# Two stores of a linear-attention kernel, each cut into three transfers of unequal height

## The chip, the core and the metric

The kernel runs on one core of one Trainium2 chip. The metric is the device time of one launch in microseconds (us). Before the change it is 127.17 us, the median of 3 runs (127.02 to 127.25).

## What is computed

Linear attention with a ReLU feature map, without softmax, in float32 at the interface: 8 x 12 = 96 heads, 512 positions, 64 features.

```python
Q_feat = np.maximum(0, Q); K_feat = np.maximum(0, K)          # (8, 12, 512, 64)
KV = np.einsum('bhkd,bhkv->bhdv', K_feat, V)                   # 64 x 64 for each head
K_sum = np.sum(K_feat, axis=2)
numerator = np.einsum('bhqd,bhdv->bhqv', Q_feat, KV)
denominator = np.einsum('bhqd,bhd->bhq', Q_feat, K_sum)
return numerator / (denominator[:, :, :, None] + 1e-10)
```

Each of Q, K, V and the output is 12.58 MB, so 37.75 MB are read and 12.58 MB written.

## The kernel before

The 96 heads are worked through in 12 "octets" of 8 heads (`NO = 12`). For an octet, Q is one tile of 128 partitions, 2048 float32 in a partition in memory; K and V are two groups of four heads each, 128 partitions x 1024. The result of an octet is the tile `o_sb`, 128 partitions x 2048 float32: a row of 8 KB per partition, 1 MB in all, which is contiguous in memory.

Loads. The first octet's K and V come as float32 through the queues of SP and ACT (`k_first`, `v_first`, lines 109 and 110). All other loads are issued by GpSimd (lines 94 and 106) and cast to bf16 on the way; they are written out in one list at the top (K, V, Q of octet 1, of octet 2, and so on) and run as far ahead as their buffers allow (6 octets of K and of V, 7 of Q) and as far as eight completion semaphores, taken in turn, let them.

Compute. For each octet TensorE forms K'V and the sums of K (line 152), ScalarE and VectorE take them out of PSUM (162), Q is transposed (173) and passed through ReLU (181, 179), the numerator is formed transposed (203), copied (205) and transposed back (230), the denominator is formed beside it (212 to 224), and `norm` (236) multiplies by the reciprocal into `o_sb`. The order of the engines' instructions is written out by hand.

Stores. `store` (line 242) issues them from SP, one transfer of 128 rows for each octet (line 249), except for the last octet, whose tile goes out as two halves of its columns (line 247), each as soon as its `norm` is done. SP does nothing else after its first load. Stores are held back: the store of octet `o` is made to wait, beside its own `norm`, until the K load of octet `o + DELAY` has landed (`DELAY = 6`), so stores 0 to 5 stand behind loads 6 to 11:

```python
        st = nc.sync.dma_start(out=Ov, in_=o_sb)
        if o + DELAY < NO:
            tc.add_manual_dep(st.ins, k_load[o + DELAY].ins.name, after_load, reason="store after load")
```

SP takes its transfers' completion semaphores in turn from eight; a transfer waits until the last user of its semaphore has landed. `o_sb` comes from a pool of `DELAY + 2 = 8` buffers, of which `k_first` and `v_first` take two at the start, so the tile of octet 8 is written only after store 0 has landed, that of octet 9 after store 1.

Of the kernel before, what the change touches and what calls it, by code (L numbers as in the profile page):

```python
# [10 lines left out]
def kernel(  # L11
# [7 lines left out]
    nc = tc.nc  # L19
    B, H, S, D = Q.shape  # L20
    assert D == 64
    P = 128
# [9 lines left out]
    NO = NG // 2  # L32
    assert NO * 8 == NH and R == 16 and RQ == 32
    DELAY = 6

    fp32 = mybir.dt.float32
    bf16 = mybir.dt.bfloat16
# [3 lines left out]
    def pool(name, bufs, **kw):  # L41
        return ctx.enter_context(tc.tile_pool(name=name, bufs=bufs, **kw))
# [6 lines left out]
    rcp = pool("rcp", 2)  # L49
    outp = pool("outp", DELAY + 2)  # L50
    otp = pool("otp", 2)
# [37 lines left out]
    k_load = {}  # L89
    after_load = mybir.DependencyInfo(mybir.DependencyClass.Sync, mybir.DependencyReason.DATA)  # L90
# [151 lines left out]
    def store(o, o_sb):  # L242
        Ov = Or[o].rearrange("p (r d) -> p r d", d=D)
        if o == NO - 1:
            for j in range(2):
                rs = slice(RQ // 2 * j, RQ // 2 * (j + 1))
                nc.sync.dma_start(out=Ov[:, rs], in_=o_sb[:, rs])
            return
        st = nc.sync.dma_start(out=Ov, in_=o_sb)
        if o + DELAY < NO:  # L250
            tc.add_manual_dep(st.ins, k_load[o + DELAY].ins.name, after_load, reason="store after load")

    def out_tile():
        return outp.tile([P, RQ, D], fp32, name="o_sb", tag="o_sb")
# [19 lines left out]
    def backs(o):  # L274
        o_sb = out_tile()
        for j in range(2):
            norm(o, j, back(o, j), o_sb)
        store(o, o_sb)
# [26 lines left out]
    o = NO - 2  # L305
# [10 lines left out]
    o_sb = out_tile()  # L316
# [4 lines left out]
    for i in range(2):  # L321
        relu_q(o + 1, i, transp(o + 1, i), nc.vector if i == 1 else None)
    norm(o, 1, ps, o_sb)
    store(o, o_sb)
    idle(5, o + 1)
    out_t(o + 1, (0,))
# [32 lines left out]
```

## Time and profile before

| | us |
|---|---|
| median of 3 runs | 127.17 (127.02 to 127.25) |
| profiled execution, device time | 127.0 |
| its span, first to last instruction | 125.2 |
| outside the span | 1.8 |
| store 0 issued on SP | 51.74 |
| store 1 issued on SP | 61.67 |
| last two stores issued on SP | 118.23 and 119.36 |

| engine | busy us | share of the span |
|---|---|---|
| TensorE matmuls | 85.0 | 68% |
| VectorE | 81.0 | 65% |
| ScalarE | 79.0 | 63% |
| GpSimd | 23.7 | 19% |
| the 16 DMA engines, mean, in 38 of 40 slices | | 90% or more |

The page cuts the span into 40 equal slices of 3.1 us. The row "DMA" gives the mean busy share of the core's 16 DMA engines in tenths (9 stands for 90% or more), the row below it what they moved. A queue's line gives its packets, megabytes, and the time that its packets took as a share of 16 engines' span: 0.4% is 0.004 x 16 x 125.2 = 8 us of one engine's time.

The trace also holds a record for each DMA packet (start, duration, size, queue, but not which engine carried it) and for each landing of a transfer: 49 transfers have 784 landing records, 16 each.

### The profile page before, as it was taken

Reading aid. Unit: us, or ns where it says so; the run is one execution under the profiler, and the core shown is the slowest. Engines: PE = TensorE matmul, PEld = TensorE weight load, DVE = VectorE, ACT = ScalarE, POOL = GpSimd, SP = SyncE. Lnnn points to the kernel's source line nnn. Section 1 sums busy time; section 2 is a strip of 40 time slices with the busy share of each in tenths; the row PEclk is TensorE's granted clock in tenths of the full one; section 3 lists DMA queues with packets and bytes.
Section 4 is the critical chain, followed back from the end, with each engine's and each line's share of the span. In section 5 each row is a group of like instructions: output and inputs, shape, how many; then the busy total and the mean of one; then the engine's idle time right before and its main releaser. Section 6 shows DMA issues by size and latency. Waiting matters only on the chain.

```text
span 125.2 us, 2614 instructions
## 1 busy us (share of the span) xinstructions
PE 85.0 (68%) x1067; PEld 76.9 (61%) x1067; DVE 81.0 (65%) x176; ACT 79.0 (63%) x114; POOL 23.7 (19%) x40
## 2 busy tenths in 40 slices
PE   0000547898989979898966985955997597797600
PEld 0000547796878879787855983943975595775500
DVE  2006963679889797979859349449549409978610
ACT  0003737999899898989877576845499095547000
POOL 6922124221242213322121130210000000000000
PEclk9999999999999999999999599996899869999996
DMA  3999999999999999999999999999999999999991
GB/s 92 365 306 229 215 209 211 213 211 217 207 217 208 211 213 211 214 273 311 214 247 341 210 222 342 234 217 325 258 215 305 279 215 307 425 419 419 432 403 73
DMA packets 10139, 32.66 MB, mean 261 GB/s; under 512 B 784, under 2 KB 784, under 8 KB 8720
## 3 DMA queue, kind: packets, MB, share of 16 engines
q0 software_dynamic: 7712, 17.83, 74.1%
q1 hardware_dynamic: 2144, 13.63, 27.1%
q10 hardware_dynamic: 272, 1.05, 2.2%
q8 instruction: 8, 0.13, 0.4%
q14 instruction: 3, 0.02, 0.0%
HBM read 37.75 MB, written 12.58 MB: 402 GB/s over the span
## 4 chain that ended last, share of the span: by engine, by line
DVE 37%; DMA 28%; PE 19%; ACT 7%; issue 3%; DVEq 1%; ACTq 0%
DMA v_sb<-in_V_dram 20%; DVE o_sb L236 15%; PE ps_kv L152 10%; DMA k_first<-in_K_dram 7%; DVE kf L138 7%; PE ps_bk L230 7%; DVE vo L140 4%; ACT kvd L162 3%; DVE vo L147 3%; DVE den L220 2%; PE ps_qt L173 2%; DVE rec L224 2%; DVE own L215 2%; ACT qt L181 2%; ACT vo L145 1%
## 5 line engine op out<-in xcount | busy, mean ns | idle before, releaser
L152 PE MATMUL ps_kv<-vo,kf 128*128 128x132 bf16 x384 | 30.2, 240 | 19.9 <-ACT vo L145 13.8
L152 PEld LDWEIGHTS <-kf 128*128 128x128 bf16 x384 | 27.4, 107 | 21.6 <-DVE vo L140 12.9
L236 DVE TENSOR_TENSOR o_sb<-ps_bk,rec 128x1024 f32<-128x1024 f32 x24 | 28.3, 1219 | 13.6 <-PE ps_bk L230 13.6
L162 ACT CAST kvd<-ps_kv 64x260 bf16<-64x260 f32 (+1 forms) x54 | 18.6, 345 | 16.6 <-PE ps_kv L152 13.9
L205 ACT COPY ot_sb<-ps_ot 128x1024 f32<-128x1024 f32 x24 | 24.1, 1013 | 6.8 <-PE ps_ot L203 5.9
L230 PE MATMUL ps_bk<-ident,ot_sb 128*128 128x128 f32 x192 | 23.4, 276 | 0.4 <-ACT ot_sb L205 0.4
L181 ACT ACTIVATE qt<-ps_qt 128x1024 bf16<-128x1024 bf16 x23 | 22.4, 1028 | 0.2
L230 PEld LDWEIGHTS ps_bk<-ident,ot_sb 128*128 128x128 f32 x192 | 21.2, 143 | 0.7 <-ACT ot_sb L205 0.7
L203 PE MATMUL ps_ot<-qt,kvd 128*128 128x256 bf16 x96 | 14.9, 283 | 9.9 <-DVE o_sb L236 9.0
L138 DVE TENSOR_SCALAR kf<-k_sb,mask 128x1024 bf16<-128x1024 bf16 x44 | 18.4, 459 | 4.5 <-DMA k_sb<-in_K_dram 4.5
L203 PEld LDWEIGHTS <-kvd 128*128 128x128 bf16 x96 | 9.2, 100 | 13.2 <-issue 11.0
L173 PE MATMUL ps_qt<-ident,q_sb 128*128 128x128 bf16 x192 | 14.7, 237 | 0.7 <-DMA q_sb<-in_Q_dram 0.7
L173 PEld LDWEIGHTS <-q_sb 128*128 128x128 bf16 x192 | 13.3, 108 | 1.4 <-DMA q_sb<-in_Q_dram 1.3
L140 DVE TENSOR_SCALAR vo<-v_sb,mask 128x1024 bf16<-128x1024 bf16 x22 | 11.0, 501 | 4.7 <-DMA v_sb<-in_V_dram 4.7
L145 ACT ACTIVATE vo<-v_sb,mask 128x1024 bf16<-128x1024 bf16 x10 | 11.5, 1154 | 2.0 <-DMA v_sb<-in_V_dram 1.8
L94 POOL DMA_DIRECT2D v_sb<-in_V_dram x11 | 8.2, 750 | 22.2 <-DMA q_sb<-in_Q_dram 9.4
L106 POOL DMA_DIRECT2D q_sb<-in_Q_dram x12 | 7.1, 588 | 20.9 <-DMA k_sb<-in_K_dram 15.3
L94 POOL DMA_DIRECT2D k_sb<-in_K_dram x11 | 7.9, 717 | 15.4 <-DMA v_sb<-in_V_dram 9.8
L212 PEld LDWEIGHTS <-qt 128*128 128x128 bf16 x192 | 6.8, 96 | 3.6 <-ACT qt L181 2.5
L212 PE MATMUL ps_den<-kvd,qt 128*128 128x16 bf16 x192 | 7.3, 180 | 1.9 <-ACT qt L181 1.7
L145 ACT ACT_TABLE_LOAD x1 | 1.3, 1283 | 11.3 <-DMA v_first<-in_V_dram 11.3
L138 DVE TENSOR_SCALAR kf<-k_first,mask 128x1024 bf16<-128x1024 f32 x4 | 2.8, 750 | 7.7 <-DMA k_first<-in_K_dram 7.7
(24 smaller groups left out, 31.8 us busy)
## 6 DMA issues: line engine op xcount, KB each, us to landing
out_dram<-o_sb SPq DMA_DIRECT2D x11, 1024.0 KB, 8.9
q_sb<-in_Q_dram POOLq DMA_DIRECT2D x12, 512.0 KB, 20.7
k_sb<-in_K_dram POOLq DMA_DIRECT2D x11, 512.0 KB, 21.8
v_sb<-in_V_dram POOLq DMA_DIRECT2D x11, 512.0 KB, 20.5
k_first<-in_K_dram SPq DMA_DIRECT2D x1, 1024.0 KB, 9.3
v_first<-in_V_dram ACTq DMA_DIRECT2D x1, 1024.0 KB, 10.5
out_dram<-o_sb SPq DMA_DIRECT2D x2, 512.0 KB, 4.5
```

What stands on the lines that cost most here:

```text
L94: ld = eng.dma_start(out=t.rearrange("p g r d -> p g (r d)"), in_=X[2 * o:2 * o + 2].rearrange("g p f -> p g f"))
L138: nc.vector.tensor_scalar(kf[g][:, :, s, :], k_sb[g], scalar1=0.0, scalar2=mask[:, 0, s:s + 1], op0=Alu.max, op1=Alu.mult)
L140: nc.vector.tensor_scalar(vo[g % NB][:, :, 0, 2:D + 2], v_sb[g], scalar1=mask[:, 1, 0:1], scalar2=None, op0=Alu.mult)
L152: nc.tensor.matmul(ps_kv[:, g % 2, 0:2 * (D + 2)].rearrange("p (t d) -> p t d", t=2), kf[g][:, r, :, :].rearrange("p s d -> p (s d)"), vo[ ...
L162: copy(kvd[o % NK][64 * c:64 * c + 64, 4 * gs.start + s:4 * gs.stop:2, c * D1:c * D1 + D1].rearrange("p (g t) d -> p g t d", t=2), ps_kv[6 ...
L173: nc.tensor.transpose(ps[:, u, :], q_sb[o][:, i * (U // 2) + u, :], ident)
L181: nc.scalar.activation(to, ps, Act.Relu)
L203: nc.tensor.matmul(ps[:, i], kvd[o % NK][:, h, 1:2 * D + 1], q[:, :, h, :], start=True, stop=True, skip_group_check=True)
L205: nc.scalar.copy(ot[o][:, :, 4 * j:4 * j + 4], ps.rearrange("p h u c -> p u h c"))
L212: nc.tensor.matmul(ps[:, u], qt_sb[o % NZ][:, u, :], kvd[o % NK][:, :, 0:2 * D1:2 * D1 - 1], start=True, stop=True, skip_group_check=True)
L230: nc.tensor.transpose(ps[:, 2 * v:2 * v + 2].rearrange("p c d -> p (c d)"), ot[o][:, 8 * j + v].rearrange("p h c -> p (h c)"), ident32)
L236: nc.vector.tensor_tensor(o_sb[:, rs], ps, rec[o][:, rs].unsqueeze(2).to_broadcast([P, 16, D]), op=Alu.mult)
```

## The change

The stores of octets 0 and 1 are each cut along the partitions into three transfers, issued one after the other on SP: 112, 8 and 8 rows for octet 0; 112, 12 and 4 rows for octet 1. All other stores stay as they are. Each piece is given the same dependence on the K load of `o + DELAY`. The purpose that the change states is that low-numbered DMA engines carry more rows than high-numbered ones.

```diff
     DELAY = 6
+
+    SPLIT = {0: (112, 8, 8), 1: (112, 12, 4)}
...
-        st = nc.sync.dma_start(out=Ov, in_=o_sb)
-        if o + DELAY < NO:
-            tc.add_manual_dep(st.ins, k_load[o + DELAY].ins.name, after_load, reason="store after load")
+        at = 0
+        for n in SPLIT.get(o, (P,)):
+            st = nc.sync.dma_start(out=Ov[at:at + n], in_=o_sb[at:at + n])
+            at += n
+            if o + DELAY < NO:
+                tc.add_manual_dep(st.ins, k_load[o + DELAY].ins.name, after_load, reason="store after load")
+        assert at == P
```

In the built program the streams of TensorE, ScalarE and GpSimd are unchanged. SP issues 17 transfers instead of 13 after its first load; of three pieces only the first carries the wait for the K load and for `norm`, the other two follow it directly. The `norm` of octet 8 waits for three completion semaphores where it waited for one, and so does that of octet 9. As SP takes four semaphores more, some later stores wait for other transfers than before (store 4 for the first piece of store 0, store 10 for store 2); the last two wait for stores 3 and 4 as before.

## The prediction

> **What bounds the kernel now.** I read the page's rows by slice first, because a change to stores can only matter if the DMA engines matter.
>
> ```profile
> DMA  3999999999999999999999999999999999999991
> GB/s 92 365 306 229 215 209 211 213 211 217 207 217 208 211 213 211 214 273 311 214 247 341 210 222 342 234 217 325 258 215 305 279 215 307 425 419 419 432 403 73
> q8 instruction: 8, 0.13, 0.4%
> ```
>
> The 16 DMA engines are busy from the second slice to the last but one, while no compute engine passes 68% of the span. The third line is a small queue that will carry the argument: 8 packets of 16 KB, in which the chip fetches instructions. Their 0.4% of 16 engines' 125.2 us is 8 us, so about 1 us each (in the packet records 0.88 to 0.97 us). They come at 27, 37, 48, 58, 71, 83, 98 and 112 us.
>
> Next the stages, to see whether the end is compute or the draining of stores (columns: busy us and count of each engine, clock, DMA share, GB/s), and the last issues on SP.
>
> ```profile
> 100.00:107.00 7.00, 5.63 (x58) 5.12 (x57) 3.82 (x6) 5.22 (x8) 0.00 (x0) 0.82 1.08 272
> 107.00:120.00 13.00, 9.50 (x115) 8.38 (x114) 9.80 (x18) 4.87 (x10) 0.00 (x0) 1.00 1.01 423
> 120.00:122.00 2.00, 0.00 (x0) 0.00 (x0) 0.00 (x0) 0.00 (x0) 0.00 (x0) 1.00 0.98 404
> ```
>
> ```profile
> 118.23 1.46 SPq L247 DMA_DIRECT2D out_dram<-o_sb  x2
> ```
>
> From 107 us on only stores move, at 423 GB/s with all engines full; compute is over at 119.3 us and the last store is issued at 119.36. From issue to first packet an idle queue took 1.07 us (`k_first`: issued at 0.74, first packet at 1.81), and a half tile takes an engine 1.25 us (8 packets of 156 ns). An engine without backlog would thus end at 119.36 + 1.07 + 1.25 = 121.68. The actual ends are in the DMA rows from 120 to 126 us (40 slices of 0.15 us):
>
> ```profile
> DMA  9998899999998767554421000000000000000010
> GB/s 492 382 437 355 355 410 382 410 437 410 410 410 328 300 273 273 218 218 191 164 109 55 27 0 0 0 0 0 0 0 0 0 0 0 0 0 0 0 55 0
> ```
>
> The engines do not stop together: they drop out one after the other from 121.8 to 123.5 us. The last engine sets the end: its landing is recorded at 123.89, and 1.3 us later the span is over. So the kernel ends when the most loaded DMA engine has worked off its share.
>
> **Which engine is last, and why.** The records do not name a packet's engine, but an engine's packets follow each other closely: one starts 3 to 22 ns before the end of the one before it. Following the packets from the end of the run backward, with the known order of each engine's transfers (8 rows per 1 MB store and one 4-byte completion, and so on), gives 16 chains without an idle gap of more than 25 ns from 13 us to the end. All 16 carry the same data at the same pace (a 2 KB load packet takes 173 ns on nearly all of them). Their ends differ by the fetches: each of the eight hits another chain. The eight chains without one end at 121.80, 121.82, 121.86, 121.91, 122.10, 122.32, 122.53 and 122.74; the eight with one at 122.94, 122.94, 123.02, 123.09, 123.23, 123.23, 123.35 and 123.56. The landing records agree: behind each fetch one more of a load's 16 landings is about 1 us late.
>
> What moves per row: within the draining stage an 8 KB row starts 306 ns after the one before it (309 ns long, 3 ns overlap). As no engine idles, a row taken off an engine at 52 or 62 us ends that engine's work 0.31 us earlier at 123 us, and a row added ends it 0.31 us later.
>
> **The change part by part.**
> Rows. Before, each engine carries 8 rows of each store. If a transfer is spread by number from engine 0 up, one row in turn, 112 rows are 7 on each engine, 8 rows are one on engines 0 to 7, 12 one on 0 to 11, 4 one on 0 to 3. Over both stores engines 0 to 3 carry 9 + 9 = 18 rows (+2, +0.61 us), 4 to 7 carry 9 + 8 = 17 (+1, +0.31), 8 to 11 carry 7 + 8 = 15 (-1, -0.31), 12 to 15 carry 7 + 7 = 14 (-2, -0.61). The trace has no transfer of fewer than 128 rows, so this spread is an assumption. The Trainium skill ("DMA: Bandwidth & Descriptors", section on why a DMA increments its semaphore by 16) says the same for the queues of SP and ACT: the largest count up to 16 that divides the rows, on the lowest-numbered engines; no run here shows it yet.
>
> Are the eight late engines the high-numbered ones? `k_first` is issued to idle engines, and their first packets start one after the other, 1.81 to 2.04 us, some 14 ns apart. If that order is the engines' number, the last nine starters are engines 7 to 15. Followed back to there, 6 or 7 of these nine are late chains and only 1 or 2 of the first seven. Chains cross between 3 and 13 us, where some links are guesses, so I take this as evidence and not as proof: three chances in four.
>
> Then the eight late chains gain 0.31 or 0.61. The latest, 123.56, ends at 123.25 if it is one of engines 8 to 11 and at 122.95 if not. The other eight lose 0.31 or 0.61: the one at 122.74 ends at 123.05 or 123.35, the one at 122.53 at 122.84 or 123.14. The last engine thus ends between about 123.0 and 123.35 instead of 123.56: a gain of 0.2 to 0.55 us. I take 0.4, the middle.
>
> Issue. Four more transfers on SP at 0.33 us each (row of the stores, 332 ns), 1.3 us in all. They stand behind stores 0 and 1 on a queue whose next own wait, for the K load, lasts until 61.7 and 71.6 us: nothing late. SP waits 98.5 us for K loads in all, which is the cover; without it the price is 0.33 us each. Completion packets: 4 bytes, 6 to 22 ns each, two to four more on an engine, under 0.1 us. Waits: the `norm` of octets 8 and 9 waits for three landings instead of one, but store 0 landed at 60.7 and store 1 at 69.7, over 20 us before those tiles are written, and VectorE's queue behind them isn't touched. The semaphores taken in turn by stores 4 and 10 belong to transfers that landed tens of us before.
>
> A rule against the change: the same page of the skill advises (section "Rules for kernel authors") against splitting into small transfers, with a fixed cost of about 2 us each. If that occupied the engines, four transfers would cost some 8 us (an estimate from that page). The row speaks otherwise: with engines always full, a transfer's end occupies an engine for one packet of 6 to 22 ns.
>
> Slower rows. Seven partitions per engine instead of eight may make engines meet at the same partitions' path. No row shows it; the nearest are rows of 326 to 361 ns that one chain showed while draining, against 309. With 14 rows at 0.03 to 0.05 us that is 0.4 to 0.7 us at most on an engine and perhaps nothing; I take nothing and keep 0.1 to 0.2 for the range.
>
> Compute. Loads land when the slowest engine lands, so earlier late engines bring the wait for the V load that ends at 83.97 forward by up to 0.3 us. The last store may be issued that much earlier; but the end is set by backlog, 123.56 against 121.68, so this pays nothing more.
>
> **Sum.** Profiled execution: 127.0 (span 125.2, 1.8 around it), less 0.4 is 126.6. The median of the runs is 0.17 above the profiled one: 127.17 - 0.4 = 126.77, about 126.75. Less than 0.2%, 0.25 us, is about what a measurement of this kernel can't tell from no change (three runs span 0.23 us).
>
> **Rivals.**
> Wrong half (17%): the late engines are the low-numbered ones, or a mixture. For it: the chains' early links. Against: 6 or 7 of 9. The last chain gains 1 or 2 rows: 123.56 + 0.31 to 0.61, so 127.5 to 127.8, slower. It decides as soon as the chain that ends at 123.56, or one within 0.3 us of it, is among engines 0 to 7.
> Not spread (8%): the small transfers go over one engine, or slow rows down. One engine with 7 + 8 + 8 rows of store 0 carries 15 more, 4.6 us, which even on the earliest chain passes the end by 2.8 us: 130 us or more. Mild forms end near 127.2 to 127.5.
> Compute bound (within the first case): if the end hung on the last issue at 119.36, balancing would give nothing, 127.2. The drain view speaks against it: 1.9 us lie between 121.68 and 123.56.
>
> **How the numbers follow.** Planned spread with late high engines: 75%, of which 60 exceed 0.25 us (gains of 0.2 to 0.55, small costs off), 14 lie within, 1 is slower. Wrong half: 17%, of which 14 slower and 3 within. Not spread: 8% slower. Faster 0.60, same 0.17, slower 0.23. Range: 126.45 (gain of 0.55 plus 0.17 of run scatter) up to 127.55, which takes in the weaker half of the wrong-half case; what is left out is under 2 in 10. The likeliest case's own range is 126.45 to 127.05.
>
> **What would show it.** Right: the DMA rows from 120 us on stay full longer and then fall in about 1.3 us instead of 1.75, the queue of SP counts four transfers of 32 to 112 rows more, the last landing comes near 123.5, and the instruction queue still has 8 packets of about 1 us. Wrong: the fall is longer than before (wrong half), a single engine's tail after 124 (not spread), or idle DMA slices before 121 us. A fetch that falls on other engines from run to run would undo the forecast too.

## The result and the profile after

The change makes the kernel slightly slower: 127.34 us, the median of 12 runs (127.23 to 127.57), against 127.09 (12 runs of the kernel before, taken beside them). The ratio is 1.0021, its 95% interval 1.0012 to 1.0029. The forecast was 126.75, a gain of 0.4 us. The profiled execution took 127.23 us with a span of 125.44 (before: 127.0 and 125.21), so it shows the loss at its full size: 0.23 us.

From the page after, the rows by slice of the DMA engines and the queues (packets, MB, share of 16 engines' time):

```profile
DMA  3999999999999999999999999999999999999991
...
q1 hardware_dynamic: 2176, 13.63, 26.8%
...
q8 instruction: 8, 0.13, 0.4%
q14 instruction: 3, 0.02, 0.0%
```

The engines are as full as before and the eight large instruction fetches are there. The queue of SP and its kin (q1) has 32 packets more than the 2144 of before. Four transfers that reached all 16 engines would add 64 completion packets; 32 is 8 + 8 + 12 + 4, one for each row of the small pieces. The line of q14, three small instruction fetches of 8 KB, also stood on the page before, and the prediction passed over it.

The pieces in the list of DMA issues after (transfers, KB each), and then, from the landing records, how many landings each left:

```profile
out_dram<-o_sb SPq DMA_DIRECT2D x2, 896.0 KB, 8.1
...
out_dram<-o_sb SPq DMA_DIRECT2D x2, 64.0 KB
out_dram<-o_sb SPq DMA_DIRECT2D x1, 96.0 KB
out_dram<-o_sb SPq DMA_DIRECT2D x1, 32.0 KB
```

```
112 rows: 16 landings        8 rows:  8 landings and 1 record at its issue (52.74 us)
                            12 rows: 12 landings and 1 record at its issue (62.72 us)
                             4 rows:  4 landings and 1 record at its issue (63.06 us)
```

So the spread over k engines is as the prediction assumed. It is what the Trainium skill ("DMA: Bandwidth & Descriptors", section on why a DMA increments its semaphore by 16) states, with the count that the rows divide; that the k engines are the lowest-numbered is that page's word alone, since no record names an engine. Below, "engines 0 to 3" means the four that carry two rows more, and so on.

The stages after 100 us, in the same columns as before:

```profile
100.00:107.00 7.00, 5.71 (x63) 5.18 (x61) 3.75 (x6) 5.16 (x8) 0.00 (x0) 0.85 1.08 267
107.00:120.00 13.00, 9.50 (x115) 8.38 (x114) 9.87 (x18) 4.93 (x10) 0.00 (x0) 1.00 1.02 425
120.00:122.00 2.00, 0.00 (x0) 0.00 (x0) 0.00 (x0) 0.00 (x0) 0.00 (x0) 1.00 0.97 397
```

Nothing has moved in the stages (423 GB/s became 425). The draining end, DMA rows from 120 to 126 us after:

```profile
DMA  6989999999999878642221000000000000000001
GB/s 273 437 355 464 410 410 437 382 437 410 437 410 382 328 328 355 273 191 109 109 82 82 0 0 0 0 0 0 0 0 0 0 0 0 0 0 0 0 0 55
```

The engines stay full some 0.3 us longer and then fall more steeply, in about 1.3 us. That is the sign that the prediction named for "right". Yet the last landing is recorded at 123.88, where it was at 123.89. The last engine's data did end 0.10 us earlier (its last packet of a store ends at 123.46, before at 123.55), but the landing is recorded 0.43 us behind that packet, where it was 0.34 before and is 0.33 to 0.36 in the traces of the experiments. For the rest, only the middle moved together.

**Where 0.23 us were lost: behind the last landing.** What SP waits for from 100 us on, before and then after (total us, times, longest):

```profile
SPq L354 <- DMA out_dram<-o_sb: 3.8, 3, 1.4
```

```profile
SPq L360 <- DMA out_dram<-o_sb: 4.0, 3, 1.6
```

Line 354, 360 after, issues nothing: it is the end of the program, where SP waits for every DMA completion semaphore before its first `DRAIN` instruction. The single records of that line, taken from the trace (start us, semaphore waited for; each record names a second one besides, left out here):

```
before: last store -> semaphore 117, last landing 123.89
  106 119.742 | 108 119.811 | 109 119.873 | 113 119.937 | 114 119.998 | 115 121.433 | 116 122.704 | 117 123.907
  118 123.968 | drain 124.033
after:  last store -> semaphore 113, last landing 123.88
  106 119.808 | 108 121.445 | 109 122.677 | 113 123.899
  114 123.961 | 115 124.020 | 116 124.082 | 117 124.141 | 118 124.203 | drain 124.268
```

The order is fixed, and each wait takes about 0.061 us though its semaphore is long complete. Transfers take the semaphores in turn. Before, the last store's was the last but one, so one wait stood behind it; with four transfers more it takes a semaphore four places further on in the turn of eight, which is near the front of the order, and five waits stand behind it. From last landing to first drain it is 0.143 us before and 0.385 after. The difference, 0.24 us, is as large as the whole loss: the last landing has not moved, so all of the loss lies behind it. That the last landing has not moved is itself a balance of two effects, as the experiments show.

### The profile page after: what moved, and what is told of

The parts are those of the page before. It is cut to its first block, busy times and chain, and to the rows that moved or that the text cites. A ratio compares the mean times of both kernels' runs of the same rounds, so it can differ in the third digit from the quotient of the medians.

```text
span 125.4 us, 2620 instructions
## 1 busy us (share of the span) xinstructions
PE 85.0 (68%) x1067; PEld 77.4 (62%) x1067; DVE 81.2 (65%) x176; ACT 78.9 (63%) x114; POOL 23.5 (19%) x40
## 4 chain that ended last, share of the span: by engine, by line
DVE 39%; DMA 28%; PE 20%; ACT 5%; issue 2%; DVEq 1%; ACTq 0%
DMA v_sb<-in_V_dram 20%; DVE o_sb L238 17%; PE ps_kv L154 10%; DMA k_first<-in_K_dram 7%; PE ps_bk L232 7%; DVE kf L140 7%; DVE vo L142 4%; DVE vo L149 3%; DVE den L222 2%; ACT kvd L164 2%; PE ps_qt L175 2%; DVE rec L226 2%; DVE own L217 2%; ACT qt L183 2%; DVEq L360 1%
## 5 line engine op out<-in xcount | busy, mean ns | idle before, releaser
L154 PE MATMUL ps_kv<-vo,kf 128*128 128x132 bf16 x384 | 31.0, 244 | 20.8 <-ACT vo L147 13.8
L154 PEld LDWEIGHTS <-kf 128*128 128x128 bf16 x384 | 28.2, 109 | 22.3 <-DVE vo L142 12.9
L205 PE MATMUL ps_ot<-qt,kvd 128*128 128x256 bf16 x96 | 14.0, 271 | 9.2 <-DVE o_sb L238 8.5
```

Of the source, the lines that this page charges most:

```text
L154: nc.tensor.matmul(ps_kv[:, g % 2, 0:2 * (D + 2)].rearrange("p (t d) -> p t d", t=2), kf[g][:, r, :, :].rearrange("p s d -> p (s d)"), vo[ ...
L205: nc.tensor.matmul(ps[:, i], kvd[o % NK][:, h, 1:2 * D + 1], q[:, :, h, :], start=True, stop=True, skip_group_check=True)
```

## Experiments

All kernels replace the store of one transfer by a loop over pieces; each is named by its two tables (columns are in units of 64 float32, 32 to a row). Tables that are not given are empty. After the first kernel the diffs show the table alone.

```diff
-        st = nc.sync.dma_start(out=Ov, in_=o_sb)
...
+        at = 0
+        for n in ROWS.get(o, (P,)):
+            c0 = 0
+            for c in COLS.get(o, (RQ,)):
+                st = nc.sync.dma_start(out=Ov[at:at + n, c0:c0 + c], in_=o_sb[at:at + n, c0:c0 + c])
...
```

In the table, "gap" is the time from the last landing to SP's first drain, "landing" the last landing, both in the profiled execution; "behind" is the number of waits behind the last store's. The gap is also called the exit. The kernel before ran at 126.98 to 127.02 us beside these runs, but at 127.09 beside the change, so the ratios compare better than the times.

| kernel | transfers more | behind | gap us | landing us | median us | ratio (95%) |
|---|---|---|---|---|---|---|
| before | 0 | 1 | 0.143 | 123.89 | 127.0 | 1 |
| the change | 4 | 5 | 0.385 | 123.88 | 127.34 | 1.0021 (1.0012 to 1.0029) |
| one_more | 1 | 0 | 0.082 | 123.80 | 127.13 | 1.0006 (0.9996 to 1.0016) |
| two_more | 2 | 7 | 0.511 | 123.83 | 127.46 | 1.0043 (1.0030 to 1.0057) |
| cols_4more | 4 | 5 | 0.385 | 124.42 | 127.75 | 1.0073 (1.0043 to 1.0103) |
| rows_lane | 8 | 1 | 0.143 | 124.53 | 127.66 | 1.0046 (1.0034 to 1.0058) |
| rows_lane_8k | 8 | 1 | 0.143 | 123.83 | 127.00 | 1.0004 (0.9995 to 1.0012) |
| rows_balanced | 4 | 5 | 0.384 | 123.43 | 126.87 | 0.9990 (0.9981 to 0.9998) |
| one_more_8k | 1 | 0 | 0.081 | 123.56 | 126.56 | 0.9962 (0.9948 to 0.9975) |
| low4_last | 9 | 0 | 0.081 | 124.15 | 127.23 | 1.0022 (1.0013 to 1.0030) |
| rows_bal_lane | 8 | 1 | not read | not read | 126.75 | 0.9981 (0.9972 to 0.9990) |
| low4_four | 16 | 1 | not read | not read | 130.36 | 1.0267 (1.0253 to 1.0281) |
| one_later | 1 | 0 | 0.082 | 123.62 | 126.68 | 0.9968 (0.9947 to 0.9988) |
| nine_more | 9 | 0 | 0.081 | 123.58 | 126.63 | 0.9969 (0.9956 to 0.9981) |
| no_cut | 0 | 1 | 0.143 | 123.97 | 127.06 | 1.0004 (0.9994 to 1.0013) |
| one_drain | 1 | 0 | 0.081 | 124.81 | 127.59 | 1.0049 (1.0033 to 1.0065) |
| lane_half | 8 | 1 | 0.142 | 123.74 | 126.86 | 0.9988 (0.9978 to 0.9998) |
| lane_nine | 9 | 0 | 0.081 | 124.16 | 127.19 | 1.0013 (1.0005 to 1.0022) |
| one_more_8k_again | 1 | 0 | 0.081 | 123.65 | 126.50 | 0.9963 (0.9950 to 0.9977) |
| one_later_again | 1 | 0 | 0.082 | 123.74 | 126.62 | 0.9970 (0.9958 to 0.9982) |

The profiled executions of rows_bal_lane and low4_four took 428.41 and 136.12 us, far from their medians, so their traces are not read.

### Is it the place of the last store's semaphore?

**one_more** and **two_more** cut store 0 by columns, so that no engine's rows change.

```diff
+    COLS = {0: (16, 16)}
```

> Store 0 as two column halves of 128 rows: one transfer more, so the last store takes the semaphore that SP waits for last of all. Exit theory: one wait fewer behind the last landing than before, -0.06 us, about 127.03, which the rounds may not tell from no change; in the profile 0.06 us less between the last landing and SP's last drain. Row theory, and a theory that each further transfer costs something by itself: no change, or +0.02 to +0.06 us.

```diff
+    COLS = {0: (16, 8, 8)}
```

> Store 0 as three column pieces of 128 rows: two transfers more, so the last store wraps around to the first of SP's eight completion semaphores. Exit theory: six more waits of 0.061 us follow its landing than before, +0.37 us, about 127.46, more than the change lost although only two transfers were added. Theory that each further transfer costs something (0.06 us each, as +0.25 for four would give): +0.12 us. Row theory: no change.

The gaps came as the order of waits says: no wait behind gives 0.082 us, seven give 0.511, and the steps fit 0.061 us each (0.082 + 7 x 0.061 = 0.51). The waits of SP in two_more, which is stuck at one semaphore to the end and then goes through seven:

```profile
SPq L364 <- DMA out_dram<-o_sb: 5.5, 1, 5.5
```

One transfer more is free here, two cost 0.46 us, of which the exit is 0.37 (0.511 less 0.143). The gain of 0.06 that one_more should show is not seen (127.13 against 127.0): cutting by columns has a price of its own, as the next two kernels show.

**cols_4more** was to give the change's four transfers without its moved rows, **rows_lane** the change's rows with the wheel turned on by four more.

```diff
+    COLS = {0: (16, 8, 8), 1: (16, 8, 8)}
```

> Stores 0 and 1 go out as three column pieces each, all of 128 rows: four transfers more, as in the change, but every DMA engine carries the bytes that it carried before. Exit theory: at the end SP waits for the completion semaphores one by one, some 0.06 us each, in a fixed order; four transfers more move the last store to a semaphore that stands four places earlier in that order, so four more waits follow its landing. That gives +0.24 us over the kernel before (127.09 becomes about 127.33), as large as the whole loss of the change. Row theory: the loss comes from rows that were moved onto engines which end late; with rows balanced the time is that of before, within 0.05 us.

```diff
+    ROWS = {0: (112, 8, 8), 1: (112, 12, 4)}
+    COLS = {2: (8, 8, 8, 4, 4)}
```

> The change's row pieces in stores 0 and 1, and store 2 cut into five column pieces of 128 rows: eight transfers more in all, so the last store takes the same completion semaphore as before the change. Exit theory: the end sequence is as short as before, what is left is the effect of the moved rows, which the two traces put at 0 to -0.2 us: 126.9 to 127.1. Row theory: the rows are as in the change, so the loss stays: +0.25 us, about 127.34.

The gaps are those of five waits and of one, but both ended about 0.5 us too late: pieces of columns make packets of 4, 2 or 1 KB instead of 8. Counted as time, the bytes that all engines together had moved fall behind those of before by 0.1 to 0.17 us after a store in halves (one_more), by about 0.25 after each store in 16, 8 and 8 (cols_4more), and by 0.5 to 0.6 after the one in five pieces (rows_lane), and never catch up. These two runs are confounded and decide nothing more.

**rows_lane_8k** repeats rows_lane with whole rows in store 2.

```diff
+    ROWS = {0: (112, 8, 8), 1: (112, 12, 4), 2: (32, 32, 32, 16, 16)}
```

> The change's row pieces in stores 0 and 1, and store 2 in five balanced row pieces (32, 32, 32, 16, 16): eight transfers more, whole 8 KB rows, so the last store takes the same completion semaphore as before the change. Exit theory: the end sequence is as short as before and what remains is the moved rows: 0 to -0.2 us, 126.85 to 127.1. Row theory: +0.25 us, 127.34.

Its DMA rows from 120 to 126 us:

```profile
DMA  9799999999999878543200000000000000000200
```

The change's moved rows with the exit of before run at 127.00, before at 127.02, and the gap is 0.143 again. With the exit of before the loss is gone: that the change pays 0.24 us at the exit is shown. And the moved rows, together with the cuts that move them, bring nothing of the 0.4 us forecast: the fall is steep, but the last landing stays at 123.83. Rows and cuts are taken apart further below.

### Why do the moved rows bring nothing?

The change makes engines distinguishable in the trace: a chain of packets can only belong to engines 0 to 3 if it carries two rows more, and so on. With this the 16 chains of the profile after can be put into four groups, most probably so (the assignment of one fetch, at 70.5 us, is open between the last two groups):

```
engines     rows  end of the last data packet, us           instruction fetches
0 to 3      +2    122.42  122.46  122.80  123.46            the three of 8 KB, at 29, 49 and 119 us
4 to 7      +1    122.09  122.67  123.07  123.34            two of 16 KB, at 48 and 58 us
8 to 11     -1    121.76  122.69  122.81  123.35            three of 16 KB, at 71, 84 and 98 us
12 to 15    -2    121.86  122.68  122.71  122.81            three of 16 KB, at 27, 37 and 112 us
```

Six of the eight large fetches are on the upper half, two on engines 4 to 7; engines 0 to 3 have none, but they have the small ones. The small one at 119 us costs 0.31 us for itself and 0.35 for the slow row right behind it (662 ns instead of 309); behind the one at 49 us no slow packet shows. The engine that ends last, at 123.46, is the one of engines 0 to 3 with the fetch at 119 us: without its two rows it would end at 122.85 (123.46 less 0.61). The latest engine got 0.10 us earlier, a former early one took its place, and the mean of the 16 ends hardly moved (122.65 before, 122.69 after).

The table also shows an order: taken by time, the large fetches go round the engines, 48 and 58 us on engines 4 to 7, then 71, 84 and 98 on engines 8 to 11, then 112 on engines 12 to 15, where those at 27 and 37 us had been too. The traces of rows_lane_8k and lane_nine, read in the same way, show the same round with another start (on engines 4 to 7 the fetches at 27 and 37 us in the one, at 70 and 83 in the other). Each time two fall on engines 4 to 7, three on each of the upper groups and none on engines 0 to 3. Which fetch an engine gets thus differs between these traces; how many each group gets does not.

**low4_last** was to use this: rows of store 0 to engines 0 to 3 alone, which seemed free of fetches, and the last store's semaphore at the end of the order.

```diff
+    ROWS = {0: (112, 4, 4, 4, 4), 1: (32, 32, 16, 16, 16, 16)}
```

> Store 0 as 112, 4, 4, 4, 4 rows, so engines 0 to 3 carry three rows more and all others one less, and store 1 as six balanced row pieces (32, 32, 16, 16, 16, 16): nine transfers more, so the last store takes the semaphore waited for last. The trace of the change put no instruction fetch on engines 0 to 3 and all eight on 4 to 15. If so, these twelve engines end 0.31 us earlier, the first four 0.92 later (at 122.7 to 123.1): the last landing moves from 123.9 to about 123.6, and with 0.06 us less at the exit the time is -0.2 to -0.4 us, about 126.75. If the fetches fall elsewhere (on engines 0 to 3 too), the last landing moves to 124.5 or later and the time is +0.5 us.

It ran at 127.23, and this reason fell. Its DMA rows from 120 to 126 us show a single engine's tail:

```profile
DMA  9698989999989887754120000000000000000002
```

That engine is one of engines 0 to 3 with the small fetch at 110.8 us, ending at 123.81; the three others of its group end at 122.76 to 123.17. The small fetches in the table above were taken into account only after this run.

**low4_four** measures the price of a row on these engines at a large dose.

```diff
+    ROWS = {0: (112, 4, 4, 4, 4), 1: (112, 4, 4, 4, 4), 2: (112, 4, 4, 4, 4), 3: (112, 4, 4, 4, 4)}
```

> Stores 0 to 3 each as 112, 4, 4, 4 and 4 rows: engines 0 to 3 carry 11 rows of each, twelve more than before in all, and engines 4 to 15 carry 7, four fewer. Sixteen transfers more, the last store's semaphore as before (0.14 us). If a row is worth 0.306 us on its engine wherever it was moved, engines 0 to 3 end 12 x 0.306 = 3.67 us later than the 121.8 to 122.9 at which they end without moved rows: chain ends 125.5 to 126.5, last landing 125.8 to 126.9, a time of 129.0 to 130.0 us. The DMA row from 122 us on then stays near a quarter (four of 16 engines) for some 3 us. If the small transfers were spread otherwise or rows could be made up for elsewhere, the time stays below 128.5.

Twelve rows cost 3.36 us of time, 0.28 us each; if the latest of these engines would otherwise end 0.7 us before the last, as in the table of chains, it is (3.36 + 0.7) / 12 = 0.34. Against the evenly cut rows_bal_lane of the next section (126.75) the two figures are 0.30 and 0.36. The price of 0.306 lies within all this. A row added to an engine is paid in full at the end of the kernel.

### Against cuts that move no row

**rows_balanced** and **one_more_8k** cut along rows in multiples of 16, so that every engine still has 8 rows of each store.

```diff
+    ROWS = {0: (64, 32, 32), 1: (64, 32, 32)}
```

> Stores 0 and 1 as row pieces of 64, 32 and 32: four transfers more as in the change, whole 8 KB rows as in the change, but heights that sixteen divides, so every DMA engine should carry eight rows of each store as before. This is the cut of column pieces again without their smaller packets, which had cost DMA time by themselves. Exit theory: the last landing comes as before (123.9 us in the profile), four more waits of 0.061 us follow it: +0.24 us, 127.25 to 127.35. Row theory: rows are balanced, so the time is that of before.

```diff
+    ROWS = {0: (64, 64)}
```

> Store 0 as two balanced row halves of 64: one transfer more, so the last store takes the semaphore that SP waits for last. Exit theory: one wait of 0.061 us fewer behind the last landing, -0.06 us. Row theory, and a price per transfer: no change or +0.06 us.

The exits are as computed (0.384 and 0.081), but both kernels are about 0.4 us faster than the exit alone would make them: 127.02 + 0.24 is 127.26 for the first, which ran at 126.87, and 127.02 - 0.06 is 126.96 for the second, which ran at 126.56. So the baseline for the moved rows is not the uncut store but the evenly cut one. rows_balanced is the twin of the change itself: same number and place of transfers, same exit, only the rows of stores 0 and 1 even. It runs at 0.9990 of before and the change at 1.0021, so the moved rows cost some 0.4 us here. Its DMA rows from 120 to 126 us:

```profile
DMA  9889999999987556552100000000000000001000
```

Its last landing is at 123.43, that of the change at 123.88, that of before at 123.89. The last landing of the change stands still because an even cut brings it forward by 0.46 us and the unevenness takes 0.45 of that back. So the loss of 0.24 us has the exit as its place, but not as its only remedy: with the exit of before the changed rows run at 127.00, and with even rows the longer exit is more than made up, at 126.87.

Two further pairs of twins were run in the same way. rows_bal_lane is the twin of rows_lane_8k, lane_nine that of nine_more, and lane_half has one store of each.

```diff
+    ROWS = {0: (64, 32, 32), 1: (64, 32, 32), 2: (32, 32, 32, 16, 16)}
```

> Stores 0 and 1 as 64, 32 and 32 rows and store 2 as 32, 32, 32, 16 and 16 rows: eight transfers more, so that the last store has the same completion semaphore as in the kernel before and the same number of waits behind it (0.14 us from the last landing to the first drain). It is the twin of rows_lane_8k (127.00 us), with the same number and place of transfers, but every engine carries 8 rows of each store. If the unevenly moved rows cost what separates the change from the balanced cut (about 0.4 us), this runs at 126.6 us and its last landing comes near 123.4. If the moved rows neither cost nor gain, it runs at 127.0 like its twin, and the 0.4 us of the balanced cut belongs to something else.

```diff
+    ROWS = {0: (64, 32, 32), 1: (64, 32, 32), 2: (32, 32, 32, 16, 16), 3: (64, 64)}
```

> The cuts of rows_bal_lane and of one_later together: nine transfers more, every engine 8 rows of each store, the last store's semaphore last in the order of waits (0.08 us). If each balanced cut of a store brings 0.4 us by itself, this falls to 126 us or below; if one cut brings the 0.4 once, 126.55; if the cuts bring nothing, 126.95. It is the candidate for a version that beats both kernels.

```diff
+    ROWS = {0: (112, 8, 8), 1: (112, 12, 4), 2: (32, 32, 32, 16, 16), 3: (64, 64)}
```

> The change's two uneven cuts, with store 2 as 32, 32, 32, 16 and 16 rows and store 3 as 64 and 64: the twin of nine_more (126.63 us), same number and place of transfers, exit of 0.08 us, but with the change's moved rows. If the moved rows cost about 0.25 us against the balanced cut, 126.9; if nothing, 126.63; if they gained what was forecast, 126.2 to 126.4.

```diff
+    ROWS = {0: (64, 32, 32), 1: (112, 12, 4), 2: (32, 32, 32, 16, 16)}
```

> rows_bal_lane with store 1 alone cut unevenly, 112, 12 and 4 rows: engines 0 to 3 carry one row more than before, 4 to 11 none, 12 to 15 one fewer; eight transfers more and the exit as before (0.14 us). If moved rows cost by what the last of engines 0 to 3 gains (0.31 us on an engine that would end some 0.3 us or more below the last one), this stays at 126.75 like its balanced twin. If an uneven cut costs by itself, whatever its size, 127.0. If the cost goes with the rows moved, midway, 126.9.

The moved rows cost 0.25 us in the first pair (127.00 against 126.75) and 0.56 in the second (127.19 against 126.63); half the dose costs 0.11 (126.86 against 126.75). The draining rows from 120 to 126 us of the second pair, nine_more and then lane_nine:

```profile
DMA  9798999999898676555320000000000000020000
```

```profile
DMA  9898989999799996643211100000000000000001
```

nine_more falls early and slowly, and is over a little after 123 us. lane_nine stays full longer and ends in a thin tail of three engines. By their rows these are one of engines 0 to 3 with the small fetch at 110.8 us (end 123.81) and two of engines 4 to 7 with the large fetches at 70 and 83 us (123.45 and 123.50); engines 8 to 15 are done by 122.97. In the change's own trace the fetches on engines 4 to 7 were those at 48 and 58 us, but the tail has the same members: the engines that got rows and have a fetch as well. The engine of 0 to 3 with the late small fetch is the last in all five traces in which the rows tell it apart: 123.46 (the change), 123.48 (rows_lane_8k), 123.40 (lane_half), and 123.81 (lane_nine and low4_last). Whether the start of the round of fetches belongs to the built program or to the execution was not tried.

### Where do the even cuts gain from?

This was not settled. **one_later** moves the cut to store 3, **no_cut** has the loop but no cut, **one_drain** cuts a store that goes out when only stores are left.

```diff
+    ROWS = {3: (64, 64)}
```

> Store 3 instead of store 0 as two transfers of 64 rows, one transfer more, with the last store's semaphore last in the order of waits (0.08 us, 0.06 less than before). one_more_8k, the same cut at store 0, ran at 126.56, 0.46 below before, of which the exit explains 0.06. Theory 1, a cut along whole rows speeds the stores' traffic: 126.55 here too. Theory 2, the remaining 0.4 comes of when the cut is made or which engine then happens to take which fetch: anything between 126.6 and 127.0, with another order of fetched engines. Theory 3, nothing but the exit: 126.96.

```diff
+    ROWS = {}
```

> The written-out loop over pieces with every store left whole: the same instructions as the kernel before, only other line numbers. Every theory expects 127.0 us here, within 0.1; what it tells apart is in its trace. If the last DMA engine to finish again ends near 123.5, is the one that carried the instruction fetch at 98 us, and was already about 0.2 us behind the mean of the engines at 15 us, the kernel before has a fixed unlucky pairing of start and fetch. If another engine is last or the start differs while the time is the same, the 0.3 us of the balanced cuts do not come from that pairing.

```diff
+    ROWS = {9: (64, 64)}
```

> Store 9, which goes out near 102 us when only stores are left, as two transfers of 64 rows; one transfer more, the last store's semaphore last in the order of waits (0.08 us). Everything before 102 us has the transfers of the kernel before. If a cut helps by what its packets do while loads and stores share the engines, only the exit is left: 126.94 us. If any additional transfer of whole rows brings the 0.3 us (by the program's length, the place of its instruction fetches or the start), this runs at 126.6 to 126.7 as the cuts of stores 0 and 3 did.

one_later gains as much as one_more_8k (126.68), no_cut nothing (127.06), so the gain comes with a cut and not with the line numbers. nine_more, with four stores cut, gains no more than one cut: it comes once. In no_cut the last engine is again the one that was fetched for at 98 us. one_drain went the other way: 127.59 in place of 126.6 or 126.94. Its trace has eleven rows of 0.46 to 1.37 us that start between 116.0 and 118.8 us, where a row takes 0.31, and a long tail in the rows from 120 to 126 us:

```profile
DMA  9969798999898887866633211110000000000000
```

Nothing in the trace says what slowed them, so this run tells nothing about the question it was made for.

A trace of one_later is already 0.39 us ahead of before at the issue of store 0 (51.35 against 51.74), before any transfer differs. That pointed to the start: the 16 landings of octet 1's V load near 16 us lie 0.67 us apart in before, in no_cut and in the change, but 0.53 in one_more_8k, 0.36 in nine_more, 0.32 in rows_balanced and 0.27 in one_later; the first packets of `k_first` are slow by different amounts on different engines. The two repeats tested it.

> one_more_8k once more: store 0 as two transfers of 64 rows. In its first trace the 16 landings of the second octet's K load, near 16 us, lay 0.53 us apart, in the kernel before 0.67, in one_later 0.27. If the spread of the engines at the start belongs to the built program, it is 0.5 to 0.55 again and the time 126.5 to 126.65. If it is drawn anew in every execution, the spread lies anywhere from 0.25 to 0.85 while the time stays, and the start does not explain the 0.4 us.

> one_later once more: store 3 as two transfers of 64 rows. If the start belongs to the program, the 16 landings near 16 us lie 0.25 to 0.3 us apart again and the time is 126.6 to 126.75; if it is drawn anew, the spread differs from 0.27 by 0.15 or more.

The spread near 16 us was 0.33 where it had been 0.53, and 0.41 where it had been 0.27 (the expectation names the K load; it is the V load of the same octet), while the medians repeated to 0.06 us (126.50 and 126.62). The spread belongs to the execution and does not set the time. The early issue of store 0 did not repeat either: 51.65 us in one_later_again. What remains true is that the evenly cut kernels end with a less late last engine, 123.1 to 123.4 against 123.56 and 123.63 in before and no_cut (one_drain apart, which ends at 124.48); the mean of the ends differs less, 122.4 to 122.7 against 122.65 and 122.7. Why a cut does that stays open.

## Why the prediction was wrong

- **Bound and price of a row: right.** The DMA engines are full to the end and the last one sets it. A row moved is 0.31 us on its engine 60 us later; twelve rows gave 3.36 us. Rows of transfers with seven partitions on an engine were no slower, the term that was kept for the range: nearly all rows of stores 0 and 1 take 322 ns, before and after.
- **Spread: right.** 8, 8, 12 and 4 landings.
- **Issue: right.** The pieces take 0.28 to 0.39 us each on SP and nobody is late for them; the stages did not move. Nor does a price of some 2 us for a small transfer show: rows_balanced, with four transfers more, ran no slower than before. (The 2 us that the prediction gives beside the rule on small transfers stand, on the same page of the Trainium skill, in the section on the anatomy of one DMA, and there for transfers issued by GpSimd.)
- **Waits: the step that failed for the measured loss.** The prediction followed the turn of the semaphores to stores 4 and 10, found their former users long landed, and put the cost at nothing. It took "1.3 us later the span is over" as a constant and did not ask which semaphore the last store takes. The term is (waits behind after less waits behind before) x 0.061 us = 4 x 0.061 = 0.24 us, and everything for it stood in the trace of before: the order at the end, and the last store's place in it.
- **Which engines are late: the step that failed for the missing gain.** "The eight late chains" were taken as the high half, at three chances in four. Six of eight were, which is what its own evidence had said (6 or 7 of nine), but the sum then took all eight. The two on engines 4 to 7 got a row on top of their fetch (123.07 and 123.34 after). The step "the other eight lose 0.31 or 0.61", with ends of 123.05 to 123.35, did not look at the small fetches; the engine of 0 to 3 that carries the late one, some 0.65 us, ended at 123.46, past the worst of these ends. Read against the uncut kernel the rows gained 0.10 us on the last engine where 0.2 to 0.55 was forecast, and nothing in the median (rows_lane_8k). Against an even cut they lose 0.25 to 0.56.
- **A fetch costs more than its packet.** It was taken at about 1 us. One costs 0.88 to 0.97 for itself and 0.3 to 0.5 more in slow packets behind it, some 1.3 us. As the ends in the prediction were read from the trace, its sum does not rest on this. The Trainium skill ("Runtime: NRT & Kernel Launch", section on instruction fetch mechanics) calls the crossing of a 16 KB block mostly hidden. Whether the engine that fetches has to wait was not looked at here; on DMA engines without an idle gap the fetch is paid for at the end.
- **Rivals.** "Wrong half" is the nearest: "a mixture" is what the trace shows. Against the uncut kernel the mixture made the rows worth nothing and not a loss of 0.3 to 0.6; against the even cut, which the prediction did not think of, it is a loss of that size. The 0.24 us at the exit had a cause that no rival named. The steep fall of the DMA rows, named as a sign of "right", appeared without any gain: it tells that the middle engines have drawn together and says nothing on the last. That the time still lies below the upper end named, 127.55, is luck: that end was put there for rows on late engines, and the 0.24 us came from the exit.

The best version of these is one_more_8k, store 0 as two transfers of 64 rows: 126.56 and again 126.50 us, 0.9962 and 0.9963 of the time before. Only 0.06 us of its 0.46 to 0.48 is explained.

## What to carry to other kernels

When a change adds or removes DMA transfers, find which semaphore the last transfer gets and how many waits stand behind it at the end of the program; a gain of a few tenths of a microsecond can be lost there, or won by one transfer more or less. Before balancing queues by hand, list everything that lands on them, the small instruction fetches too, and find out which engine carries what before moving rows, not only how many are late. Compare such a cut with an even cut of the same count, not only with the uncut kernel.

## What the runs showed of the hardware

- SP ends a program by waiting for every DMA semaphore in a fixed order, about 0.061 us for each even when it is long complete: 0.08 us after the last landing with none behind, 0.14 with one, 0.385 with five, 0.51 with seven.
- A large instruction fetch (16 KB) takes about 1.3 us from one DMA engine, the late small one (8 KB) about 0.65. In the four traces in which rows tell the engines apart (the change, rows_lane_8k, lane_half, lane_nine), no large fetch was found on engines 0 to 3 where it could be assigned, and the last small one was on one of them. The large ones go round the other engines: two on engines 4 to 7, three on 8 to 11 and three on 12 to 15 in the three traces that tell these groups apart.
- Cutting a 1 MB store along whole rows of 8 KB costs the DMA engines nothing that shows; cutting it by columns into pieces with 4 and 2 KB rows costs about 0.25 us.
- The first packets of the first load take 0.53 to 0.86 us on some engines in the trace of before. The engines' spread at 16 us, 0.27 to 0.83 us, changes from one execution to the next without showing in the time; it does not simply follow the slow first packets, since the widest, in rows_lane_8k, stands beside first packets of at most 0.45 us.
